# The scan of the odd layer in a two-block transformer kernel: block-diagonal tiles replaced by single 64 x 64 products on quarters of TensorE

## The chip, the cores and the metric

The program runs on one core of a Trainium2 chip. The metric is the device time of one execution in microseconds (us). The engines are TensorE (PE, with its weight loads as PEld), VectorE (DVE), ScalarE (ACT), GpSimd (POOL) and SyncE (SP, which issues the DMAs). The order of each engine's instructions is fixed when the program is built; between engines they wait on semaphores.

## What is computed

Two blocks of two layers follow each other, 512 tokens of x and 256 of context, 1024 features. The layer that matters here is the odd layer of the first block. Half of its mixer is an RWKV-7 recurrence over 8 heads of 64 features, once forward and once backward, first over the context and then, from the state that this leaves, over x:

```python
def wkv7_scan(state0, p, d, reverse, emit):
    ...
    def step(S, inp):
        w_t, k_t, v_t, kk_t, a_t = inp[:5]
        sa = jnp.einsum('bhvk,bhk->bhv', S, kk_t)
        S = (S * w_t[:, :, None, :] - sa[..., None] * (kk_t * a_t)[:, :, None, :]
             + v_t[..., None] * k_t[:, :, None, :])
        return S, (jnp.einsum('bhvk,bhk->bhv', S, inp[5]) if emit else None)
```

The decay `w_t` and the rate `a_t` come from low-rank products of the tokens; the outputs of both directions are added, normed per head, and gated (`rwkv7_readout`). Both kernels compute this in chunks of 64 tokens: within a chunk the steps become triangular 64 x 64 matrices per head, one of which has to be inverted, and between chunks only the 64 x 64 state passes.

## The kernel before, in words

`odd` runs the layer: the neighbourhood attention, then `rwkv_inputs` (projections, left in DRAM as `kap_d`, `k_d`, `r_d`, `vtok_d`), then `rwkv` (L1360), which holds the scan and the output product behind it. `others` gives steps of the output product of the attention half (`more`), matmuls of L414 on 512 columns, which `rwkv` spreads over the start of the scan.

**Units.** One unit is one chunk of one direction: 12 chunks (4 of context, 8 of x) times 2 directions, 24 units, each over all 8 heads. A unit is a generator, `pre` and then `serial`, that gives up its turn at every `yield`. The loop at the end of the scan goes by ticks: at every sixth tick a new unit joins, and in every tick each live unit does its next step. This order, as the tile framework's scheduler then refines it, is the order on the engines. A unit has 19 steps, so about three are live.

**Layouts.** Eight 64 x 64 matrices (one per head) are either a stack, tile [128, 4, 64], two heads on the two partition halves, or the diagonal blocks of a bd tile [128, 4, 128] whose other blocks stay zero. `prod` multiplies four stacked pairs by four bd tiles: stationary 128 x 64, moving 128 x 128. So an operand of the next product must be written into a bd tile, by two instructions of 64 partitions each (`expand` at L1401, on ACT or POOL; L1516, L1521, L1543 and L1552 likewise). `turn` (L1417) transposes a stack by two products with the identity.

**One unit.** `pre` loads kap, k and r of its 64 tokens, makes decays and scaled keys on POOL, DVE and ACT (tiles `ld`, `L`, `E`, `em`, `av`, `b`, `kd`, all 256 columns wide; the running sum is L1457), the low-rank products (L1446, tanh in `th`) once per two chunks. It then forms A (L1489) and the first inverse X (L1493, L1494), B, rk, rb, kt and bt, and inverts by five doubling levels: X is transposed to T (L1417, L1502), A is multiplied by X (masked into `bdw`, L1543), T by that, and half of X is updated (L1549) and copied to its bd tile (L1552). `values` loads the tokens' values three ways. `serial` takes the state N: products with E and B give `bdr` (L1582, L1583), X times it gives `un` (L1588), `kt` and `bt` give the new state (L1595 to L1604), and for x the output goes to `y`.

**Memory for results.** PSUM holds six one-bank tiles `rw` for `pre` and two `mm` for `serial`. At the start every bd tile is cleared (L1386, on POOL and DVE).

**After the scan** `readout` norms and gates the outputs; its first half starts at tick 141, beside the last units, the rest after them; the output product of this half follows.

Of the kernel before, what the change touches and what calls it, by code (L numbers as in the profile page):

```python
# [18 lines left out]
KD = 8  # L19
# [12 lines left out]
# ---------------------------------------------------------------- layouts made on the host  # L32
# [16 lines left out]
def _rows(w):  # L49
    """output features on partitions: [tile, P, contraction]"""  # L50
    return np.ascontiguousarray(w.T.reshape(-1, P, w.shape[0]))


def _consts():
# [24 lines left out]
    c["rscan"] = c["scan"][:, :256]  # L79
# [159 lines left out]
# ---------------------------------------------------------------- the program  # L239
# [7 lines left out]
def chain(products):  # L247
    """one step sequence: what comes after each product runs beside the steps of the next"""
# [11 lines left out]
def weave(base, other, per=1):  # L260
    """all steps of both: per steps of base, then one of other"""
# [11 lines left out]
class Prog:  # L273
# [16 lines left out]
    def xs(self, k, seg):  # L290
        """feature tile k of the residual stream, columns (first, number)"""
# [3 lines left out]
    def load_c(self, name, pool):  # L295
        """a tile of small vectors or constants, found by their names"""
# [16 lines left out]
    def psum(self, es, **bufs):  # L313
        """PSUM pools of a stage: mm one-bank tiles, s2 two-bank tiles"""
# [6 lines left out]
    def weights(self, side):  # L321
        """the pool of weights, which stages share so that loads run ahead of a stage's end"""
# [3 lines left out]
    def sbuf(self, es, side="left"):  # L326
        """scratch pool of a stage"""
# [5 lines left out]
    # ---- splitting into two float32r parts: hi + lo == value exactly  # L333
# [14 lines left out]
    def mm3(self, outs, w, acts, kt):  # L348
        """outs[i] (+)= w^T act_i over kt contraction tiles, exact float32r parts; w and acts give (hi, lo)."""
# [11 lines left out]
    def dense(self, dr, kt, act, segs):  # L361
        """feature-major product: one 128-column tile of weights dr [P, kt, P]; PSUM outputs per segment."""
# [3 lines left out]
    def dense_pair(self, drs, kt, act, segss, wide=False, by_seg=False):  # L366
        """column tiles whose products alternate over the contraction tiles, as these become ready, for all segments or
# [2131 lines left out]
```

## Time and profile before

| | us |
|---|---|
| median of 3 runs | 4167.52 |
| lowest and highest | 4164.29, 4172.4 |
| span of the profiled execution | 4163.7 |
| first A of the scan (L1489) to the last | 1389.8 to 1792.2 |
| last `un` (L1588) | 1824.2 |

No run's time is noted for the profiled execution apart from its span, which lies 3.8 us below the median of the runs. A profile row names line, engine and operation; a matmul of 32-bit floats of the program stands in it as two rows of weight load and two of matmul. "128*64 128x128" reads: 128 rows and 64 columns of the array, output of 128 columns on so many partitions. Busy time of PE counts from a row's start to its modelled end, and rows overlap.

### The profile page before, as it was taken

To read this page: it belongs to the slowest core of one execution; us is meant where nothing else is said; L and a number is where in the kernel's file an instruction comes from. 1 tells how busy PE (TensorE), PEld (TensorE's weight loads), DVE (VectorE), ACT (ScalarE), POOL (GpSimd) and SP (SyncE) were. 2 spreads that over 40 slices of the span, in tenths; PEclk is the share of its full clock that TensorE was granted. 3 is DMA by queue.
4 is the path that set the end of the run, shared out by engine and by line. 5 is a ranking of instruction groups with operands and counts; after the bars stand their busy time and mean duration, and the time that the engine had idled before them with its cause. 6 is when DMAs were issued, how large, how long until landed. Compare 5 with 4: busy or idle time off the path is not lost.

```text
span 4163.7 us, 61873 instructions
## 1 busy us (share of the span) xinstructions
PE 3961.8 (95%) x24688; PEld 3214.3 (77%) x24688; DVE 2477.5 (60%) x4382; ACT 1674.3 (40%) x3238; POOL 362.2 (9%) x439
## 2 busy tenths in 40 slices
PE   7899999999999999989999998999999899989998
PEld 5677888888777677768887877888887667767887
DVE  6556555545645676776766355555457888785334
ACT  4456321212544465553224252312125577663222
POOL 0222000000010221200000000000000231220000
PEclk8999999999999999999999998999999999999999
DMA  4220233323123211134553111233333223322232
GB/s 172 87 87 32 77 112 117 119 95 100 55 84 134 72 38 44 42 105 141 177 162 99 56 48 62 91 112 115 103 113 115 97 97 121 102 81 81 92 96 86
DMA packets 187888, 397.53 MB, mean 95 GB/s; under 512 B 80336, under 2 KB 89424, under 8 KB 186704
## 3 DMA queue, kind: packets, MB, share of 16 engines
q1 hardware_dynamic: 187600, 393.58, 29.4%
q8 instruction: 195, 3.19, 0.3%
q14 instruction: 93, 0.76, 0.1%
HBM read 379.23 MB, written 14.29 MB: 95 GB/s over the span
## 4 chain that ended last, share of the span: by engine, by line
PE 48%; DVE 5%; ACT 2%; issue 1%; POOL 0%; DMA 0%; DVEq 0%; ACTq 0%; POOLq 0%
PE mm L414 11%; PE mm L355 10%; PE mm L357 10%; PE mm L359 10%; PE mm L384 2%; PE y L2372 1%; DVE cva L2098 1%; DVE wlo L336 1%; PE seg L2170 0%; PE gl L1977 0%; ACT whi L335 0%; DVE y L2297 0%; DVE yl L2301 0%; DVE ch L2341 0%; PE mm L1412 0%
## 5 line engine op out<-in xcount | busy, mean ns | idle before, releaser
L335 ACT CAST whi<-w 128x1024 fp32r<-128x1024 f32 (+2 forms) x429 | 439.2, 1025 | 1582.4 <-PE mm L357 1008.3
L336 DVE TENSOR_TENSOR wlo<-w,whi 128x1024 fp32r<-128x1024 f32 (+2 forms) x429 | 517.6, 1207 | 329.6 <-ACT whi L335 320.8
L355 PE MATMUL mm<-fhi,whi 128*128 128x512 f32 x2016 | 610.0, 356 | 0.0
L357 PE MATMUL mm<-flo,whi 128*128 128x512 f32 x2016 | 609.4, 356 | 0.0
L359 PE MATMUL mm<-fhi,wlo 128*128 128x512 f32 x2016 | 607.5, 355 | 0.0
L359 PEld LDWEIGHTS mm<-fhi,wlo 128*128 128x128 f32 x2016 | 331.3, 187 | 61.4
L355 PEld LDWEIGHTS mm<-fhi,whi 128*128 128x128 f32 x2016 | 331.4, 187 | 60.7
L357 PEld LDWEIGHTS mm<-flo,whi 128*128 128x128 f32 x2016 | 331.4, 187 | 59.3
L471 DVE SCALAR_TENSOR_TENSOR wdot<-wmod,cb 128x1024 f32<-128x1024 f32 x288 | 352.0, 1222 | 10.8 <-ACT cb L465 3.6
L622 DVE SCALAR_TENSOR_TENSOR x<-mm,mod,x 128x512 f32<-128x512 f32 (+1 forms) x214 | 131.9, 642 | 325.5 <-PE mm L359 268.7
L734 DVE TENSOR_TENSOR g<-g,mm 128x512 f32<-128x512 f32 (+1 forms) x134 | 75.5, 590 | 405.1 <-PE mm L359 396.7
L355 PE MATMUL mm<-ah,whi 128*128 128x512 f32 x972 | 294.0, 356 | 0.0
L357 PE MATMUL mm<-al,whi 128*128 128x512 f32 x972 | 293.8, 356 | 0.0
L359 PE MATMUL mm<-ah,wlo 128*128 128x512 f32 x972 | 293.0, 355 | 0.7 <-DVE wlo L336 0.7
L359 PEld LDWEIGHTS mm<-ah,wlo 128*128 128x128 f32 x972 | 159.7, 187 | 30.7 <-DVE wlo L336 1.1
L834 POOL TENSOR_SCALAR p<-p,st 128x256 f32<-128x256 f32 (+3 forms) x128 | 95.7, 748 | 1008.3 <-DVE st L833 913.2
L355 PEld LDWEIGHTS mm<-ah,whi 128*128 128x128 f32 x972 | 159.7, 187 | 29.4
L357 PEld LDWEIGHTS mm<-al,whi 128*128 128x128 f32 x972 | 159.7, 187 | 28.7
L414 PE MATMUL mm<-shi,whi 128*128 128x512 f32 x328 | 138.9, 424 | 0.2 <-DVE x L2254 0.2
L414 PE MATMUL mm<-shi,wlo 128*128 128x512 f32 x328 | 130.6, 400 | 2.0 <-DVE wlo L336 2.0
L414 PE MATMUL mm<-slo,whi 128*128 128x512 f32 x328 | 131.8, 402 | 0.0
L2098 DVE SCALAR_TENSOR_TENSOR cva<-cvb,v_ssd,cva 128x512 f32<-128x512 f32 (+1 forms) x176 | 121.0, 701 | 11.0 <-ACT cva L2096 8.8
(598 smaller groups left out, 7957.7 us busy)
## 6 DMA issues: line engine op xcount, KB each, us to landing
wmod<-wmod SPq DMA_DIRECT2D x176, 512.0 KB, 3.7
w<-wfi SPq DMA_DIRECT2D x176, 512.0 KB, 3.3
w<-ws_in SPq DMA_DIRECT2D x62, 512.0 KB, 3.4
w<-wfo SPq DMA_DIRECT2D x64, 448.0 KB, 3.4
w<-wfo SPq DMA_DIRECT2D x32, 512.0 KB, 3.5
rb<-acd SPq DMA_DIRECT2D x32, 512.0 KB, 4.1
w<-wo_in SPq DMA_DIRECT2D x26, 512.0 KB, 3.3
w<-wa_in SPq DMA_DIRECT2D x21, 512.0 KB, 3.3
```

Source lines behind the costliest of these rows:

```text
L335: self.nc.scalar.copy(hi, src)
L336: (engine or self.nc.vector).tensor_tensor(out=lo, in0=src, in1=hi.bitcast(F32), op=ALU.subtract)
L355: nc.tensor.matmul(o, whi(k), ah(k), start=s, stop=False)
L357: nc.tensor.matmul(o, whi(k), al(k), start=False, stop=False)
L359: nc.tensor.matmul(o, wlo(k), ah(k), start=False, stop=e)
L384: self.nc.tensor.matmul(o, w[:, k], x[:, k, t0:t0 + n], start=s, stop=e)
L414: self.nc.tensor.matmul(o, w[:, k], x[:, k, t0:t0 + n], start=s, stop=e)
L471: dot = nc.vector.scalar_tensor_tensor(out=t, in0=w, scalar=1.0, in1=cb[:, i], op0=ALU.mult, op1=ALU.mult, accum_out=out[:, j, i:i + 1])
L622: self.nc.vector.scalar_tensor_tensor(out=x, in0=ps, scalar=mod[:, i_g + m, i:i + 1], in1=x, op0=ALU.mult, op1=ALU.add)
L734: nc.vector.tensor_tensor(out=g, in0=g, in1=u_, op=ALU.mult)
L834: nc.gpsimd.tensor_scalar(out=p, in0=p, scalar1=l, scalar2=1.0, op0=ALU.mult, op1=ALU.mult)
L2098: nc.vector.scalar_tensor_tensor(out=acc, in0=pc[:, t:t + n], scalar=w(t), in1=acc, op0=ALU.mult, op1=ALU.add)
```

## The change

All of it is within the scan of `rwkv`, and one constant (`rscan`, the marks at which the running sum starts anew, is 512 columns wide instead of 256).

- There are no bd tiles. `prod` takes single 64 x 64 matrices: stationary 64 x 64 on one half of the array's rows and one half of its columns, moving 64 columns (32 or 128 in places). The two halves of the rows write to different PSUM banks, so a result is a pair of banks; there are three such pairs and one ring for all products of the scan. Eight products go out as two groups of four that lie on the four quarters.
- A stack has three layouts (N, T, J), which say which bit of the head's number is the partition half. A product takes two layouts and gives the third kind; `seen` is the view of the result in the order of the target's tile.
- Decays and keys are made by `block` for two chunks at once, 512 columns wide, 9 ticks ahead of the first unit that needs them. Values come in one layout (`vj`), two DMAs per block.
- The five level masks of A are applied at once on POOL (`Al`, 1280 columns). X's transpose and A times X come as one result (`tw`, 64 + 32 columns per head: only the half of X's columns that changes), copied by one ACT instruction.
- B for x holds the strict and the inclusive products in one instruction of 512 columns; kt holds both transposes.
- B times the values is made ahead (`bv`), and the state's part is taken off it on DVE.
- A unit joins at every fourth tick and has 18 steps. The readout's first half starts when step 9 of both directions is done.

```diff
-            pps = self.pool(es, "rwps", 6, space=PSUM)
+            pps = self.pool(es, "rwps", 3, space=PSUM)
...
-            bank = lambda: pps.tile([P, 512], F32, tag="rw", name="rw")
+            LAY = {"N": (2, 0, 1), "T": (1, 0, 2), "J": (0, 1, 2)}
+            pair = lambda: pps.tile([P, 1024], F32, tag="rw", name="rw").rearrange("p (b c) -> p b c", b=2)
...
-            def prod(ps, *terms):
-                for g in range(4):
-                    o = ps[HALF[g % 2], P * (g // 2):P * (g // 2) + P]
-                    for i, (L, Rb) in enumerate(terms):
-                        nc.tensor.matmul(o, L[:, g], Rb[:, g], start=i == 0, stop=i == len(terms) - 1)
+            def prod(ps, lam, mu, *terms, base=0, step=64, at=0, n=64):
+                lb, mb = LAY[lam][0], LAY[mu][0]
+                bits = [0, 0, 0]
+                for bits[3 - lb - mb] in range(2):
+                    for i, (L, Rb) in enumerate(terms):
+                        for bits[lb] in range(2):
+                            for bits[mb] in range(2):
+                                g = 2 * bits[LAY[lam][1]] + bits[LAY[lam][2]]
+                                h = HALF[bits[lb]]
+                                o0 = base + step * bits[3 - lb - mb] + at
+                                nc.tensor.matmul(ps[HALF[bits[mb]], bits[lb], o0:o0 + n], L(g)[h], Rb(g)[h],
+                                                 start=i == 0, stop=i == len(terms) - 1)
+            def seen(ps, lam, mu, base=0, step=64, at=0, n=64):
+                v = ps[:, :, base:base + 2 * step].rearrange("p b (s w) -> p b s w", s=2)[:, :, :, at:at + n]
+                return v if LAY[mu][1] == LAY[lam][0] else v.rearrange("p b s w -> p s b w")
...
+                Al = up.tile([P, 5, 4, 64], F32, tag="Al", name="Al", bufs=3)
+                nc.gpsimd.tensor_tensor(out=Al, in0=A.unsqueeze(1).to_broadcast([P, 5, 4, 64]),
+                                        in1=mk[:, d, 1:6].unsqueeze(2).to_broadcast([P, 5, 4, 64]), op=ALU.mult)
...
                 for l in range(1, 6):
-                    Ti = inverse_t()
-                    pw = bank()
-                    prod(pw, (A, bx))
-                    W = bd("w")
-                    for h in range(2):
-                        nc.vector.tensor_tensor(out=on(W, h), in0=stack(pw)[HALF[h]], in1=mask(1 - d, l)[HALF[h]], op=ALU.mult)
+                    ps = pair()
+                    prod(ps, "T", "J", (grp(X), eye), step=96)
+                    prod(ps, "T", "J", ((lambda g: Al[:, l - 1, g]), (lambda g: blk(X[:, g]))), step=96, at=64, n=32)
+                    tw = sm("tw", 3, 96)
+                    nc.scalar.copy(two(tw), seen(ps, "T", "J", step=96, n=96))
                     yield
-                    pd = bank()
-                    prod(pd, (Ti, W))
+                    ps = pair()
+                    prod(ps, "J", "T", ((lambda g: tw[:, g, 0:64]), (lambda g: tw[:, g, 64:96])), step=32, n=32)
...
-                    if l < 5:
-                        for h in range(2):
-                            nc.scalar.copy(blk(on(bx, h)), blk(X[HALF[h]]))
+                    nc.vector.tensor_tensor(out=xb, in0=xb, in1=s, op=ALU.subtract)
                     yield
...
-                if todo and tick % 6 == 0:
-                    live.append(todo.pop(0))
+            EVERY, AHEAD = 4, 9
+            for i in range(12):
+                for d in range(2):
+                    t0 = AHEAD + EVERY * (2 * i + d)
+                    if i % 2 == 0:
+                        start.setdefault(t0 - AHEAD, []).append((block, d, chunk(d, i) // 2))
+                    start.setdefault(t0, []).append((unit, d, i))
```

On PE, in the middle of the scan, the order before (names: `bdx`, `bdw`, `bdb` are bd tiles, `consts` holds the identity):

```order
L1412 MATMUL rw<-bdb_12126,E 64x128 x4
L1412 MATMUL rw<-bde_12099,b 64x128 x4
L1417 MATMUL rw<-consts,X 128x128 x2
L1412 MATMUL mm<-bdr_12110,X 64x128 x3
L1412 MATMUL rw<-bdx_12123,A 64x128 x4
L1509 MATMUL rw<-E,bdk_12128 128x128 x4
L1519 MATMUL rw<-E,bdb_12126 128x64 x4
L1412 MATMUL mm<-bdr_12110,X 64x128
L1412 MATMUL rw<-bdw_12119,T 64x128 x4
```

and the order now (`c_odd` holds the identity of 64):

```order
L1394 MATMUL rw<-tw 64x32 x16
L1438 MATMUL mm<-ru,lora 128x128
L1394 MATMUL rw<-tw 64x32 x8
L1394 MATMUL rw<-E,kd 64x128 x8
L1394 MATMUL rw<-E,b 64x64 x8
L1394 MATMUL rw<-N,E 64x64 x8
L1394 MATMUL rw<-c_odd,X 64x64 x8
L1394 MATMUL rw<-X,Al 64x32 x8
```

Products of four matmuls on 128 rows have become products of eight on 64 rows; only the low-rank products (L1438) still use all rows, and they stand singly between the others.

On DVE, a stretch of the same place before:

```order
L1543 TENSOR_TENSOR bdw_12119<-rw,rmask 64x4x64 x2
L1543 TENSOR_TENSOR bdw_12120<-rw,rmask 64x4x64 x2
L1465 TENSOR_TENSOR E<-E,kx 128x4x64
L1467 TENSOR_TENSOR b<-b,em 128x256
L1468 SCALAR_TENSOR_TENSOR kd<-av,vecs 128x256
L1481 TENSOR_TENSOR E<-E,rr 128x4x64
L1471 SCALAR_TENSOR_TENSOR kd<-kd,kk 128x256
L1549 TENSOR_TENSOR X<-X,rw 128x4x32
L1472 TENSOR_TENSOR kd<-kd,em 128x256
L1549 TENSOR_TENSOR X<-X,rw 128x32x4
```

and now, with a block's instructions in it:

```order
L1496 TENSOR_TENSOR B<-rw,rmask 128x512
L1501 TENSOR_TENSOR rb<-rw,rmask 128x256
L1541 TENSOR_TENSOR bv<-bv,rw 128x256
L1461 SCALAR_TENSOR_TENSOR kd<-av,vecs 128x512
L1462 TENSOR_TENSOR E<-E,kx 128x8x64
L1463 TENSOR_TENSOR b<-b,em 128x512
L1465 SCALAR_TENSOR_TENSOR kd<-kd,kk 128x512
L1468 TENSOR_TENSOR kd<-kd,em 128x512
L1534 TENSOR_TENSOR X<-X,rw 128x8x16
L1534 TENSOR_TENSOR X<-X,rw 128x32x4
```

The masked copies into bd tiles are gone, and the work on decays and keys stands in runs of five or six instructions of 512 columns between those that empty PSUM.

## Rows read from the trace of the kernel before

**Rows 1.** the page: span, and busy time of each engine over the whole program

```profile
span 4163.7 us, 61873 instructions
PE 3961.8 (95%) x24688; PEld 3214.3 (77%) x24688; DVE 2477.5 (60%) x4382; ACT 1674.3 (40%) x3238; POOL 362.2 (9%) x439
```

**Rows 2.** lines L1489 and L1588: ns min/median/max, first and last start, forms

```profile
L1489 ACT COPY A<-rw x24: 372/372/373, 1389.8 to 1792.2; 128x256 f32<-128x256 f32 x24
...
L1588 ACT COPY un<-mm x24: 353/372/373, 1420.9 to 1824.2; 128x256 f32<-128x256 f32 x24
```

**Rows 3.** busy time by stretch: before the first unit, first to last, the rest

```profile
core 0: us, PE busy (x) PEld busy (x) DVE busy (x) ACT busy (x) POOL busy (x), PEclk, DMA share, GB/s
1364.50:1389.80 25.30, 21.82 (x108) 16.43 (x108) 17.23 (x31) 8.43 (x16) 13.60 (x27) 1.00 0.60 163
1389.80:1792.20 402.40, 374.63 (x4173) 301.10 (x4172) 289.26 (x734) 238.42 (x678) 83.41 (x147) 1.00 0.17 39
1792.20:1824.20 32.00, 29.64 (x298) 22.00 (x297) 20.67 (x54) 16.55 (x46) 0.00 (x0) 0.95 0.22 61
```

**Rows 4.** waits, 1389.8 to 1792.2: total us, times, longest us

```profile
ACT bdx L1552 <- DVE X L1549: 34.3, 30, 2.6
DVE N L1603 <- PE mm L1597: 32.7, 18, 2.3
...
ACT T L1502 <- PE rw L1417: 23.4, 35, 1.5
```

**Rows 5.** timeline of PE, gated linear attention: start, us, line, tiles, shapes, rows

```profile
2490.30 0.28 PE L1928 MATMUL gl<-gvt,kt 64*64 64x128 f32 x2
2490.33 0.28 PE L1952 MATMUL tp<-qd,kn 64*64 64x64 f32 x4
2490.41 0.28 PE L1928 MATMUL gl<-gvt,kt 64*64 64x128 f32 x2
2490.45 0.28 PE L1952 MATMUL tp<-qd,kn 64*64 64x64 f32 x4
2490.52 0.28 PE L1928 MATMUL gl<-gvt,kt 64*64 64x128 f32 x2
...
2535.94 0.64 PE L1952 MATMUL tp<-qd,kn 64*64 64x64 f32 x16
```

**Rows 6.** timeline in the scan: a product that fills the array

```profile
1611.99 1.16 PE L1509 MATMUL rw<-E,bdk 128*128 128x128 f32 x8
```

**Rows 7.** VectorE by line: ns min/median/max, first and last start, forms

```profile
L1549 DVE TENSOR_TENSOR X<-X,rw x120: 279/289/294, 1395.5 to 1822.7; 128x128 f32<-128x128 f32 x120
L1493 DVE TENSOR_TENSOR X<-rw,rmask x24: 407/425/427, 1389.5 to 1792.0; 128x256 f32<-128x256 f32 x24
...
L1457 DVE TENSOR_TENSOR_SCAN L<-c_odd,ld x24: 684/692/882, 1384.2 to 1771.6; 128x256 f32<-128x256 f32 x24
...
L1458 DVE TENSOR_TENSOR ld<-L,ld x24: 410/436/735, 1385.5 to 1774.7; 128x256 f32<-128x256 f32 x24
```

**Rows 8.** VectorE by line and shape, whole program: busy us, mean ns, idle before

```profile
L1249 DVE TENSOR_TENSOR zs<-zc 128x512 f32<-128x512 f32 x14 | 9.6, 687 | 8.6 <-ACT zc L1247 8.6
```

**Rows 9.** ScalarE, the same view

```profile
L886 ACT COPY pt<-tp 128x384 f32<-128x384 f32 x64 | 30.5, 477 | 56.4 <-PE tp L883 56.0
...
L1448 ACT ACTIVATE th<-rw 128x512 f32<-128x512 f32 x24 | 14.2, 597 | 2.9 <-PE rw L1446 2.0
...
L1532 ACT COPY bt<-rw 128x512 f32<-128x512 f32 x22 | 12.9, 585 | 1.1
...
L563 ACT ACTIVATE rs<-rs 128x512 f32<-128x512 f32 x6 | 3.8, 631 | 0.2
```

**Rows 10.** GpSimd, the same view

```profile
L2159 POOL TENSOR_TENSOR xw<-xt,dtw 128x512 f32<-128x512 f32 x40 | 52.0, 1304 | 816.0 <-ACT xt L2124 793.2 <-PE seg L2170 20.7 <-PE tp L2289 1.8
...
L834 POOL TENSOR_SCALAR p<-p,st 128x512 f32<-128x512 f32 x32 | 23.1, 721 | 761.1 <-DVE st L833 737.3 <-DVE st L825 8.9 <-DVE mod L502 4.7
```

**Rows 11.** busy time by stretch: the end of the gated linear attention

```profile
2541.50:2565.00 23.50, 18.19 (x118) 13.98 (x117) 10.89 (x26) 5.74 (x16) 0.00 (x0) 0.50 0.21 68
```

More of the change, by code (lines that the diff above doesn't have):

```diff
@@ L78, in _consts @@
     t = np.arange(64)
-    c["rscan"] = c["scan"][:, :256]
+    c["rscan"] = c["scan"][:, :512]
     c["i64"] = np.tile(np.eye(64), (2, 1))
@@ L1421, in chunk @@
+            eye = lambda g: i64
+            state, blocks, done = {0: None, 1: None}, {}, set()
             def chunk(d, i):
@@ L1493, in pre @@
-                nc.vector.tensor_tensor(out=X, in0=stack(ps), in1=mask(1 - d, 0), op=ALU.mult)
-                nc.vector.tensor_tensor(out=X, in0=i64, in1=X, op=ALU.subtract)
-                expand(bx, X, (nc.scalar, nc.scalar))
-                yield
-                def inverse_t():
-                    ps = bank()
-                    turn(ps, X)
-                    Ti = sm("T", 3)
-                    nc.scalar.copy(Ti, stack(ps))
-                    return Ti
-                ps = bank().rearrange("p (q t) -> p q t", q=4)
@@ L1507, in pre @@
[L1507 to L1521 removed]
+                yield
@@ L1522, in pre @@
                 yield
                 if i < 11:
-                    ps = bank()
-                    turn(ps, kd)
-                    u["kt"] = sm("kt", 3)
-                    nc.scalar.copy(u["kt"], stack(ps))
-                    ps = bank().rearrange("p (q t) -> p q t", q=4)
-                    for p in range(4):
-                        nc.tensor.transpose(ps[:, p], bb[:, p], ident)
-                    u["bt"] = up.tile([P, 4, P], F32, tag="bt", name="bt", bufs=3)
-                    nc.scalar.copy(u["bt"], ps)
@@ L1619, in unit @@
-            def unit(d, i):
-                yield from pre(d, i)
-                yield from serial(d, i)
+                    ps = pair()
+                    prod(ps, "N", "T", (grp(N), e1))
+                    prod(ps, "J", "T", (v, (lambda g: B[:, g, 64:P])), (grp(un), grp(rb)), base=P)
+                    c4 = ci - 4
+                    yy = two(y[:, :, 64 * c4:64 * c4 + 64])
+                    if (c4 < 4) == (d == 0):
+                        nc.scalar.copy(yy, seen(ps, "N", "T"))
+                    else:
+                        nc.vector.tensor_tensor(out=yy, in0=yy, in1=seen(ps, "N", "T"), op=ALU.add)
@@ L1624, in readout @@
+                    nc.vector.tensor_tensor(out=yy, in0=yy, in1=seen(ps, "J", "T", base=P), op=ALU.add)
+                done.add((d, i))
             def readout(cols, yh, yl):
@@ L1635, in readout @@
                     yield
-                    pv = two(bank())
+                    pv = halves(self.bank())
                     nc.tensor.matmul(pv, self.c("bd64"), sq, start=True, stop=True)
@@ L1644, in readout @@
                     yield
-            todo = [unit(d, i) for i in range(12) for d in range(2)]
-            live, tick = [], 0
-            while todo or live:
-                if todo and tick % 6 == 0:
-                    live.append(todo.pop(0))
-                live = [u for u in live if next(u, todo) is not todo]
-                if tick in (1, 3):
-                    clear(2 if tick == 1 else 0, (nc.gpsimd,))
+            EVERY, AHEAD = 4, 9
+            start = {}
+            for i in range(12):
[4 more added lines that the diff above has]
+                    start.setdefault(t0, []).append((unit, d, i))
+            live, tick, reading = [], 0, False
+            while start or live:
+                live += [f(*at) for f, *at in start.pop(tick, ())]
+                live = [u for u in live if next(u, start) is not start]
                 if tick < 15:
@@ L1658, in rwkv @@
                     run(more)
-                elif tick == 141:
+                elif reading:
+                    next(more, None)
+                elif (0, 9) in done and (1, 9) in done:
+                    reading = True
                     yh, yl = parts()
@@ L1662, in rwkv @@
                     more = readout(slice(1, 3), yh, yl)
-                elif tick > 141:
-                    next(more, None)
                 tick += 1
```

279 lines of the change are left out of this document (118 added, 161 removed).

## Prediction

> **What bounds the kernel now.** I read the page first, then the scan alone. Over the program PE is busy 95% of the span [rows 1], but that mean belongs to the dense products and says nothing of the scan. Where the scan lies is told by two lines that occur once per unit: A is copied 24 times, first at 1389.8 us and last at 1792.2, and the last `un` starts at 1824.2 [rows 2]. Between the first and the last A lie 23 steps of 402.4 / 23 = 17.5 us. The reader is to see in the table by stretch [rows 3] that no engine is full there: DVE is busy 289.3 of 402.4 us (72%, 12.6 us per unit) and ACT 238.4 (59%, 10.4 us per unit). PE shows 374.6, but that counts each row to its modelled end: its 4173 rows, mostly half-array rows, stream in far less. The waits [rows 4] agree: ACT waits for DVE, DVE for PE, ACT for PE, none above 34.3 of 402 us. It is a loop in which about three units hand results from PE to ACT or DVE and back. So its pace follows the sum of what the fullest engine has to do, times a factor for the waiting: 12.6 us of DVE work make 17.5 us.
>
> **The change, part by part.** The counts are those of the two programs' instructions in the scan; durations are those of rows.
>
> *DVE.* Removed are 240 masked copies into `bdw`, 64 into `rk` and `rb`, and half of those of `bdr` and `bdn`. What stays: 160 instructions of 256 columns at 0.425 us (as L1493 in [rows 7]), 68.0; 120 updates of X at 0.289 [rows 7], 34.7; 16 of B and 80 of the blocks, 512 columns at 0.687 [rows 8], 66.0; 12 running sums of 512 columns, not in the trace, at most twice the 0.692 of 256 [rows 7], 16.6. Together 185.3. GpSimd will be busier (below), and the 256-column L1458 shows what a neighbour can do: least 0.410, median 0.436, most 0.735 [rows 7]. I add twice the 6% between least and median to the 66.0, 8 us; the worst row would add 52. That makes 193 us, **8.0 us per unit** against 12.6.
>
> *ACT.* 72 copies of 256 columns (A, bv, un) at 0.372 [rows 2], 26.8; 22 of kt at 0.585, 120 of `tw` at 0.477 (its width is that of L886), 24 tanh at 0.597 and 32 exponentials at 0.631 [rows 9], together 104.6; 8 of `y`, 3.0. That is 134, **5.6 us per unit** against 10.4. Gone are the copies into `bdx`, `bdb`, `bdk`, `bdr` and T.
>
> *PE.* Now 5232 products on quarters, two rows each, 10464 rows or 436 per unit. The scan has no such row, but the gated linear attention has. There 16 rows of 64 columns on two quarters of the same partition half take 0.64 us [rows 5]; less the 0.22 of a last row's end this is 0.42 / 14 = 0.030 us per row. Where both halves work, 2 + 4 + 2 + 4 rows start from 2490.30 to 2490.52 [rows 5], 0.018 each, a third of them twice as wide. So four quarters do run at once, and I take half of 0.030: 157 us, plus 3 for 256 rows of 128 columns. Rows of 32 columns still load 64 columns of weights, so I give them no gain. The 24 groups of low-rank products fill the array, at 1.16 each [rows 6], 28. That is 188, **7.8 us per unit**; at 0.030 it would be 347, 14.5.
>
> *POOL.* 24 masks of A of 1280 columns, from 1.304 for 512 [rows 10] some 3.26 each, 78; 24 scalings at 0.721 [rows 10], 17; 12 products at 1.304, 16. That is 111, 4.6 us per unit, below the others, though one mask follows a block's three instructions and may be late for the first level, by some 2 us per block at worst (3.26 + 1.30 + 0.72 against two ticks); DVE's backlog covers that.
>
> *Nothing, and what hides it.* The 25 clearings on POOL and six on DVE ran beside the products before the first unit, where PE is busy 21.8 of 25.3 us [rows 3]. These products of `more` still stand ahead of the first unit, and a block's longer chain waits beside them, so I leave the first A at 1389.8, give or take 5. The loads fall from 188 to 56 DMAs of the same or fewer bytes; the queue was not awaited and a block is loaded 9 ticks ahead. The readout and the output product keep their work.
>
> *The pace.* DVE (8.0) and PE (7.8) are now nearly level. At the share of before, 8.0 / 0.72 = 11.1 us. A second way: before, the pace lay between DVE alone, 12.6, and DVE and ACT one after the other, 23.0, at (17.5 - 12.6) / 10.4 = 0.47 of the way; now 8.0 + 0.47 * 5.6 = 10.6. Three pairs of PSUM banks instead of eight single ones let PE run ahead by three products only, and the blocks' runs of five or six wide instructions on DVE (some 4 us) hold back the copies behind them, so I take the upper one, 11.0. The ends are 8.0 (DVE never waits) and 13.6 (ACT and DVE never overlap).
>
> *The sum.* Last A: 1389.8 + 23 * 11.0 = 1642.8. From there to the last `un` before: 14 ticks of 17.5 / 6, 40.8 us at full pace, took 32.0 [rows 3], 0.78 of it. Now 15 ticks of 11.0 / 4 are 41.3, times 0.78 = 32.2. The last `un` is at 1675.0 instead of 1824.2: 149.2 us less. The span of 4163.7 [rows 1] becomes 4014.5; the median of the runs lies 3.8 above the span, so **4018 us**. In the same way 8.0 gives 3940 and 13.6 gives 4086.
>
> [...] The rows show twelve starts in 0.22 us [rows 5], one each 18 ns. [...]
>
> **Rivals.**
>
> 1. *Two rows at a time* (slower than before). The four quarters do not get going together: in `prod` the four matmuls of a group write to two banks, accumulate in turn, and wait on results that come singly, so that the rate is that of the 16 rows, 0.030 us each [rows 5]. PE then needs 14.5 us per unit and is the fullest engine: at the share of 0.72 a pace of 20.1, last `un` at 1389.8 + 462.3 + 58.8 = 1910.9, 87 us later: 4254. It decides from a pace of 16.8 on (23 + 15 / 4 * 0.78 = 25.9 paces make 434.4 us), which PE reaches at 12.1 us per unit, 0.025 us per row; if PE never waited, 14.5 would give 4109. For it: the rows of 64 columns mostly come in twos. Against it: the mixed stretch. 10%, of which 6 slower. [...]
>
> 2. *The clock.* [...] If half of the scan ran at half clock, PE would need 11.7 us per unit, at 0.72 a pace of 16.3: 1389.8 + 374.9 + 47.7, 12 us less than before, 4156. 9%.
>
> 3. *ACT and DVE in turn.* The unit's steps come in such an order that a tick's copies are all ACT's (three `tw` and A) or all DVE's (y, three X, B, rb), and the three bank pairs let neither work while the other does. Then the pace is 13.6, 4086. For it: the PSUM ring is the only store between PE and both. Against it: four or five live steps per tick from different units, and the blocks' work needs no PSUM. This is the upper part of my own case; with it that case has 78%.
>
> The last 3% are for what none of these covers.
>
> **How the numbers follow.** 4018 is the likeliest case's own value. Its ends, 3940 and 4086, hold the unknown rate of the quarters and the sharing between GpSimd and DVE; the upper one is moved to 4110 to take in rival 1 where PE never waits, and what of rival 2 lasts shorter. Some 8 in 10 lie between. About 0.2%, 8 us, is what a measurement of this kernel can tell from no change: slower by more has the 6% of rival 1 and 2% of the clock; within it lie 4%, of rival 2 mostly; faster by more has 88%.
>
> **What would show it.** In the changed kernel's lines: A 24 times some 11 us apart, the last about 1643, the last `un` about 1675; DVE some 190 us busy between, about 70%, ACT half; 16 rows of a quarter product within 0.4 to 0.5 us; a granted clock of 1.00. It is wrong in the pace if A comes 8 or 14 us apart: then the busy shares say whether an engine filled up or bank pairs were awaited (PE waiting for the copy of the product three before). Rival 1 shows as 16 rows in 0.6 us and as waits of DVE and ACT for PE's products; rival 2 as a clock of 0.50 in the scan's stretches. If the first A is later than 1395, the start was mispriced.

## The result and the profile after

The changed kernel takes **4120.99 us** (median of 4 runs, 4116.48 to 4126.67) where the kernel before takes 4167.57 (4164.29 to 4172.4): the ratio is 0.9887, 95% interval 0.9873 to 0.9901. It is faster by some 47 us. The forecast of 4018 (3940 to 4110) had the sign; the gain is under a third of the 149 us expected.

The page of the changed kernel, span and busy time (as [rows 1]):

```profile
span 4124.9 us, 72730 instructions
PE 3850.0 (93%) x30860; PEld 3149.4 (76%) x30860; DVE 2395.2 (58%) x3988; ACT 1551.8 (38%) x2814; POOL 376.9 (9%) x322
```

Its lines for A and `un` (as [rows 2]):

```profile
L1485 ACT COPY A<-rw x24: 367/372/379, 1397.5 to 1739.5; 128x256 f32<-128x256 f32 x24
...
L1546 ACT COPY un<-rw x24: 372/378/379, 1443.2 to 1773.6; 128x256 f32<-128x256 f32 x24
```

Busy time by stretch (as [rows 3]): before the first unit, first to last A, up to the last `un`, and from there to the output product:

```profile
core 0: us, PE busy (x) PEld busy (x) DVE busy (x) ACT busy (x) POOL busy (x), PEclk, DMA share, GB/s
1364.00:1397.50 33.50, 23.67 (x133) 17.78 (x131) 17.41 (x27) 9.17 (x16) 5.95 (x6) 0.90 0.55 164
1397.50:1739.50 342.00, 257.78 (x9573) 234.12 (x9565) 206.10 (x345) 117.12 (x264) 104.74 (x53) 0.79 0.11 30
1739.50:1773.60 34.10, 28.90 (x1053) 23.52 (x1048) 19.80 (x50) 14.58 (x34) 2.89 (x1) 0.85 0.13 35
1775.00:1805.30 30.30, 18.16 (x40) 10.18 (x41) 12.90 (x28) 11.07 (x26) 0.00 (x0) 0.55 0.37 122
```

A unit now comes every 342.0 / 23 = 14.9 us, not every 11.0 (before: 17.5). Against the forecast span of 4014.5 the 110 us that are missing lie so: the first A is 7.7 us late, 23 paces are 3.87 us too long each (89.0), the tail is 1.9 longer, and behind the last `un` 11.8 are lost (4124.9 - 1773.6 = 2351.3, before 4163.7 - 1824.2 = 2339.5): the readout runs at a granted clock of 0.55 there (0.88 in the 30 us behind the last `un` before). So the loss is in the pace for the most part. VectorE is busy for 206.1 us, 9.0 per unit, 60% of the stretch; no engine is full, again. The clock stands at 0.79 where it stood at 1.00.

Where VectorE's time went, by line in that stretch (busy us, mean ns, idle time before):

```profile
L1490 DVE TENSOR_TENSOR X<-c_odd,X 128x256 f32<-128x256 f32 x23 | 55.1, 2397 | 0.3
...
L1447 DVE TENSOR_TENSOR_SCAN L<-c_odd,ld 128x512 f32<-128x512 f32 x10 | 12.2, 1224 | 37.3 <-POOL ld L1444 37.3
L1461 DVE SCALAR_TENSOR_TENSOR kd<-av,vecs 128x512 f32<-128x512 f32 x10 | 12.0, 1200 | 0.0
L1452 DVE TENSOR_TENSOR ld<-L,ld 128x512 f32<-128x512 f32 x10 | 11.7, 1174 | 0.0
L1489 DVE TENSOR_TENSOR X<-rw,rmask 128x256 f32<-128x256 f32 x23 | 9.5, 414 | 31.4 <-PE rw L1394 31.4
```

L1489 and L1490 have one shape, 256 columns. The first reads PSUM and takes 0.41 us; the second reads two operands in SBUF and takes 2.40. The timeline of one unit shows why (rows of PE left out):

```profile
1520.37 2.88 POOL L1504 TENSOR_TENSOR Al<-A,rmask 128x1280 f32<-128x1280 f32 x1 [10.52 <-ACT A L1485]
...
1520.57 0.29 DVE L1534 TENSOR_TENSOR X<-X,rw 128x128 f32<-128x128 f32 x1 [0.17 <-PE rw L1394]
1520.78 2.76 DVE L1490 TENSOR_TENSOR X<-c_odd,X 128x256 f32<-128x256 f32 x1
...
1523.46 0.47 DVE L1534 TENSOR_TENSOR X<-X,rw 128x128 f32<-128x128 f32 x2
```

GpSimd's mask `Al` ends at 1523.25, the subtraction at 1523.54. In 20 of the 23 units the subtraction ends 0.3 us after the `Al` that it met. In the other three, which met none, it takes 0.41 to 0.42. L1534, with one operand in PSUM, runs through beside the mask in 0.29. So in these rows the subtraction, with two operands in SBUF, is held until the mask that it meets is done: 2.40 us in the mean against 0.41.

### The profile page after: what moved, and what is told of

Its sections match the earlier page's. It is cut to its first block, busy times and chain, and to the rows that moved or that the text cites. A ratio compares the mean times of both kernels' runs of the same rounds, so it can differ in the third digit from the quotient of the medians.

```text
span 4124.9 us, 72730 instructions
## 1 busy us (share of the span) xinstructions
PE 3850.0 (93%) x30860; PEld 3149.4 (76%) x30860; DVE 2395.2 (58%) x3988; ACT 1551.8 (38%) x2814; POOL 376.9 (9%) x322
## 3 DMA queue, kind: packets, MB, share of 16 engines
q8 instruction: 242, 3.96, 0.4%
## 4 chain that ended last, share of the span: by engine, by line
PE 52%; DVE 8%; ACT 3%; issue 2%; POOL 0%; DMA 0%; DVEq 0%; ACTq 0%; SPq 0%; POOLq 0%
PE mm L414 11%; PE mm L355 10%; PE mm L357 10%; PE mm L359 10%; PE rw L1394 4%; PE mm L384 3%; PE y L2327 1%; DVE X L1490 1%; DVE wlo L336 1%; DVE cva L2053 1%; PE seg L2125 0%; PE gl L1932 0%; PE mm L1438 0%; DVE ch L2296 0%; ACT whi L335 0%
```

## The experiments

Each ratio is to the kernel before, run on the same chip. That kernel took 4165.8 to 4172.9 us on the chips used, so kernels of different chips are compared by their ratios. Pace is from the first to the last A; clock and VectorE's busy time are those of that stretch, in one execution of each kernel. For the mask on VectorE that execution, 4091.5 us, was the slowest of four, so paces some 0.5 us apart are not told from each other.

| kernel | us | ratio, 95% interval | pace us | clock | DVE us |
|---|---|---|---|---|---|
| the change | 4121.0 | 0.9887 (0.9873 to 0.9901) | 14.9 | 0.79 | 206 |
| X from PSUM | 4103.7 | 0.9854 (0.9839 to 0.9868) | 14.1 | 0.86 | 173 |
| mask in five pieces | 4102.7 | 0.9848 (0.9832 to 0.9865) | 14.0 | 0.88 | 167 |
| **mask on VectorE** | 4080.0 | 0.9799 (0.9781 to 0.9816) | 13.25 | 0.89 | 185 |
| change + filling products | 4124.6 | 0.9902 (0.9887 to 0.9916) | 14.9 | 0.90 | 210 |
| change + later running sum | 4115.7 | 0.9875 (0.9860 to 0.9890) | 14.7 | 0.82 | 206 |
| X from PSUM + later sum | 4111.1 | 0.9863 (0.9846 to 0.9879) | 14.2 | 0.87 | 173 |
| mask on VectorE, and: | | | | | |
| - unit every 3 ticks | 4097.7 | 0.9826 (0.9812 to 0.9841) | 13.1 | 0.88 | 187 |
| - filling products | 4104.5 | 0.9847 (0.9832 to 0.9861) | 14.1 | 0.95 | 191 |
| - four PSUM pairs | 4087.4 | 0.9813 (0.9797 to 0.9830) | 13.4 | 0.89 | 186 |
| - two PSUM pairs | 4123.2 | 0.9897 (0.9882 to 0.9912) | 14.6 | 0.79 | 196 |
| - thin blocks | 4075.1 | 0.9779 (0.9759 to 0.9798) | 12.9 | 0.94 | 158 |
| - tw in bfloat16 | 4072.6 | 0.9761 (0.9747 to 0.9776) | 12.6 | 0.83 | 192 |
| - 32 tiny products | 4123.7 | 0.9886 (0.9872 to 0.9901) | 14.8 | 0.84 | 187 |
| - turns as transposes | 4393.5 | 1.0539 (1.0521 to 1.0556) | 25.8 | 0.59 | 182 |
| - tw in bfloat16, `more` spread | 4069.5 | 0.9763 (0.9748 to 0.9777) | 13.1 | 0.86 | 194 |
| before + 32 tiny products | 4231.5 | 1.0157 (1.0140 to 1.0174) | 20.2 | 0.94 | 298 |

### Is it GpSimd's hold on VectorE?

**X from PSUM.**

```diff
-vector.tensor_tensor(out=two(X), in0=seen(ps), in1=mask(1 - d, 0), op=mult)
-vector.tensor_tensor(out=X, in0=i64s, in1=X, op=subtract)
+vector.tensor_tensor(out=seen(ps), in0=seen(ps), in1=mask(1 - d, 0), op=mult)
+vector.tensor_tensor(out=two(X), in0=i64q, in1=seen(ps), op=subtract)
```

> Edit: the masked product is written back into its PSUM pair, and X is formed from that, so that VectorE's second instruction for X reads one operand from PSUM and one from SBUF, not two from SBUF. GpSimd's mask of A (Al) stays as it is. Theory 'lock' (VectorE's subtraction of two SBUF operands waits until GpSimd's Al ends, 2.4 us in the mean instead of 0.42; PE starves behind it and its clock falls afterwards): the subtraction takes some 0.42 us, VectorE's sum between the first and the last A falls from 206 to some 161 us, the granted clock there rises from 0.79 to over 0.93, the pace falls from 14.9 to 12 to 12.8 us, and the time is 4055 to 4080. Theory 'short rows' (rows on quarters keep PE too little at work for the full clock, whatever VectorE does): the subtraction gets short as well, but the clock stays at 0.75 to 0.85, the pace at 14 to 14.9, and the time is 4100 to 4121.

VectorE loses 33 us, the time 17: 4103.7 lies in the range of 'short rows', not of 'lock'. The subtraction is short, but by line, in the same stretch, another instruction with two SBUF operands now meets the mask:

```profile
L1453 DVE TENSOR_TENSOR ld<-L,ld 128x512 f32<-128x512 f32 x10 | 25.8, 2577 | 0.0
...
L1448 DVE TENSOR_TENSOR_SCAN L<-c_odd,ld 128x512 f32<-128x512 f32 x10 | 12.2, 1224 | 34.0 <-POOL ld L1445 34.0
```

The hold has moved to `ld` (2.58 us; 1.17 in the changed kernel).

**Mask in five pieces.** One instruction of 1280 columns on GpSimd becomes five of 256, each in its own tile.

> Edit: GpSimd's one mask of 1280 columns (2.9 to 3.9 us) becomes five of 256 columns, each in a tile of its own; VectorE's instructions stay. Theory 'lock': VectorE waits for one piece at most (about 0.7 us by the 256 columns' share of the 3.3), the subtraction takes 0.42 to 1.2 us in place of 2.4, and the time is 4060 to 4090. Theory 'short rows': the subtraction gets shorter too, the clock stays near 0.79, time 4100 to 4121. If the lock is handed over only when GpSimd's queue is empty, nothing changes: 4121.

The subtraction falls to 0.63 us in the mean, the time by 18 us, again into the range of 'short rows'. The hold has moved here too: `E` at L1462 takes 1.46 us in the mean.

**Mask on VectorE.** `nc.gpsimd.tensor_tensor(out=Al, ...)` becomes `nc.vector.tensor_tensor(out=Al, ...)`.

> Edit: the mask of A goes from GpSimd to VectorE, in one instruction of 1280 columns. Theory 'lock': the subtraction takes 0.42 us, the mask itself some 1.7 us on VectorE (128 columns 0.28, 512 columns 0.68, so about 0.10 us per 100 columns), VectorE's sum is some 200 us as now, but nothing waits for GpSimd; clock over 0.88, time 4080 to 4105. Theory 'short rows': VectorE does no less than now and the clock stays, 4115 to 4135.

By line of VectorE in the scan:

```profile
L1504 DVE TENSOR_TENSOR Al<-A,rmask 128x1280 f32<-128x1280 f32 x23 | 34.6, 1503 | 56.1 <-ACT A L1485 56.1
...
L1447 DVE TENSOR_TENSOR_SCAN L<-c_odd,ld 128x512 f32<-128x512 f32 x10 | 12.2, 1220 | 1.3 <-POOL ld L1444 1.3
...
L1490 DVE TENSOR_TENSOR X<-c_odd,X 128x256 f32<-128x256 f32 x23 | 10.4, 454 | 0.1
```

Best of the three, though VectorE now does the mask as well (1.50 us against 3.32 on GpSimd): the subtraction takes 0.45 us, and VectorE no longer stands before the running sum for `ld` (1.3 us in place of 37.3). The time falls by 41 us, into the range of 'lock', and the clock rises to 0.89, which 'short rows' excluded.

But two things changed at once. VectorE's wait for `ld` in the changed kernel did not come from a queue on GpSimd:

```profile
1532.93 0.60 ACT L1439 ACTIVATE th<-mm 128x512 f32<-128x512 f32 x1 [0.58 <-PE mm L1438]
...
1533.61 0.62 POOL L1444 TENSOR_SCALAR ld<-th 128x512 f32<-128x512 f32 x1 [10.36 <-ACT th L1439]
...
1534.26 1.22 DVE L1447 TENSOR_TENSOR_SCAN L<-c_odd,ld 128x512 f32<-128x512 f32 x1 [3.24 <-POOL ld L1444]
```

GpSimd had been idle for 10.36 us and began `ld` some 0.09 us after the end of the tanh that it reads, and so in all ten blocks of the stretch. VectorE stood because its order has the running sum ahead of the time when low-rank product and tanh are done. With the mask on VectorE the rest of its order is another as well, and the wait is gone. So the 41 us are the price of the hold and of this order together. Loosening the hold alone gave 17 and 18 us, with the wait for `ld` still there (34.0 and 36.9 us). The hold is shown, by three ways of loosening it; its share of the 41 us is not.

**Later running sum.** One more `yield` ahead of the running sum, on the change and on X from PSUM.

> Edit: in the block's preparation the running sum on VectorE (L1447 of the changed kernel) comes one tick later than GpSimd's scaling of ld that it reads; Al stays on GpSimd, and so does the lock on the subtraction. In the changed kernel VectorE stood 37 us in 10 waits for ld, since ld queues on GpSimd behind an Al. Theory 'queue' (VectorE, held at the running sum, holds the copies behind it): those waits fall under 10 us, and the time falls by 10 to 25 us from 4121, to 4096 to 4111. Theory 'lock alone': VectorE would have stood elsewhere in that time, 4115 to 4125.

> Edit: X formed from PSUM (as in the first experiment, 4104) and the running sum one tick later, with Al still one mask on GpSimd. Theory 'lock and queue' (the mask on GpSimd costs the scan by these two ways and by nothing else): together they give what moving the mask to VectorE gave, 4065 to 4085. If only one of them matters: 4095 to 4105. Theory 'short rows': the clock stays at half for 70 us or more of the scan, and the time over 4090.

Neither tests its theory: VectorE still waits 34.7 and 34.3 us for `ld`, presumably since the framework's scheduler sets the order anew. The edit did not do what it says, so the 4115.7 us in the range of 'lock alone' say nothing. The second kernel's 4111.1 us are in the range of 'short rows' alone, with a clock of 0.87. A queue on GpSimd, which the first text gives as the cause, is not what the rows above show.

### Is it the clock?

```diff
+fl = self.bank()
+for _ in range(2):
+    nc.tensor.matmul(fl, lora[:, 0, 0, 0:P], lora[:, 0, 1], start=True, stop=True)
```

> Edit: behind each unit's second product (the one for X) PE gets two more full-array float32 products of 512 columns into a spare bank that nothing reads; nothing else changes, so the output is the same. They take about 0.85 us each at full clock, 40 us of PE in the scan. Theory 'lock': the subtraction still takes 2.4 us and still ends with Al, the pace stays above 14, time 4100 to 4140, whatever the clock does. Theory 'short rows': the clock rises over 0.93 and PE, freed from half clock, gives a pace of 12 to 13.5, time 4060 to 4095 in spite of the added work.

> Edit: the mask of A on VectorE (4080) and two more full-array products of 512 columns behind each unit's second product, into a bank nothing reads. Half clock then still took 68 us of the scan. Theory 'clock': the clock rises to 0.96 or more and the pace falls to 11.5 to 12.5, time 4045 to 4070. Theory 'latency': the clock rises, but PE is not what is waited for, and the added work (1.7 us per unit) takes PE away from others: pace 13 to 14, time 4075 to 4105.

On the change the clock rises from 0.79 to 0.90 and the pace stays at 14.9: if the higher clock gave anything, the added products took it. Without the hold it rises from 0.89 to 0.95 and the kernel gets 24 us slower. Of the 20 times that the clock fell to half in the change's scan, 17 lie within 2 us of the end of an `Al`. That fits a clock that falls because PE has run dry behind the hold; shown is only that holding it up with idle work brings nothing. Nor do the rows on quarters by themselves hold it at 0.79, as 'short rows' had it: the same rows run at 0.89 with the mask on VectorE and at 0.94 with thin blocks.

### What sets 13.25 us, with the hold gone?

VectorE is busy 185.2 us of 304.8, of which the mask is 34.6; its other work is 6.5 us per unit in this stretch. The pace is 13.25 all the same, not 11.0. Four things were tried.

**A unit every 3 ticks** (`EVERY` 3 in place of 4).

> Edit: the mask of A on VectorE (4080) and a new unit every 3 ticks in place of 4, so that about six units are under way instead of four. Theory 'latency' (no engine is full: PE starts rows in 131 of 305 us, VectorE is busy 185, ACT 116; a tick lasts as long as the chain of one step, about 3.3 us): the pace falls by up to a quarter, from 13.25 to 10.5 to 11.5 us, and the time to 4025 to 4050. Theory 'in order' (VectorE and PE are held by their own queues, one late step holding all others): the tick grows as the steps in it do, pace 12.3 to 13.3, time 4065 to 4085.

**PSUM pairs.** Four: the ring gets the banks of `mm`, and `self.bank()` takes the first bank of a pair. Two: the ring's 3 becomes 2.

> Edit, on the kernel with the mask of A on VectorE (4080 us, pace 13.25): four pairs of PSUM banks in place of three; the two single banks of the low-rank products, of `more` and of the readout are given up, these take the first bank of a pair from the same ring. Theory 'ring' (a product starts only when the product three before has been copied out; a unit takes a pair about 20 times, and if each is held 1.7 to 2 us, three pairs give 11 to 13 us per unit): the pace falls to 10 to 11.5 us and the time to 4025 to 4050, perhaps 10 us more since `more` holds pairs at the start. Theory 'engines' (VectorE's order of work and PE's own sequence set the tick; another pair only waits longer): pace 12.8 to 13.5, time 4070 to 4090.

> Edit, on the kernel with the mask of A on VectorE: two pairs of PSUM banks in place of three, all else the same. Theory 'ring': the pace goes with the number of pairs, 17 to 20 us, time 4165 to 4235, slower than before the change. Theory 'engines': pace under 14.5, time under 4110.

**Thin blocks.** Six wide instructions of the blocks work on 8 of 64 columns.

> Edit, on the kernel with the mask of A on VectorE: six of the wide instructions of a block's preparation on VectorE work on 8 of 64 columns (64 per partition in place of 512) and leave the rest of their results out; the scaling of av is made 100 times smaller to keep the numbers bounded. VectorE loses some 0.55 us in each of 68 instructions, 36 of its 185 us. Theory 'bursts' (VectorE's runs of wide instructions, some 6 us per block, hold the copies behind them): pace 10.8 to 12, time 4020 to 4055. Theory 'ring' with a hold that has other causes: pace 12.4 to 13, time 4060 to 4075. Theory 'load' (pace goes as VectorE's sum, at the share 0.61): 6.5 / 0.61 = 10.7 us.

**Four pairs and a unit every 3 ticks.**

> Edit, on the kernel with the mask of A on VectorE: four pairs as in the first of these runs and a new unit every 3 ticks in place of 4. With three pairs the shorter distance changed the pace from 13.25 to 13.06 only. Theory 'ring': with more pairs the shorter distance counts too, pace 9.5 to 10.5, time 4005 to 4035. Theory 'engines': as with four pairs alone, or up to 20 us more as at three pairs (4098 against 4080).

The shorter distance alone takes the pace to 13.1 but lengthens the tail, and costs 18 us, more than either theory had. A fourth pair brings nothing (13.4), though it also has to serve the low-rank products, and with units every 3 ticks it brings nothing either (4101.0). A pair less costs 1.3 us per unit, a fraction of what the ring would make it; its 4123.2 us lie between the two theories. With thin blocks 27 us less on VectorE bring 0.35 us per unit and 5 us of time, within the spread of the runs (4065 to 4081). Ring, latency, bursts and VectorE's load each fail as the one bound.

What these runs share is in PE's rows. The timeline of PE, mask on VectorE, in brackets the idle time and what the profile names as its end:

```profile
1629.47 0.41 PE L1394 MATMUL rw<-c_odd,X 64*64 64x64 f32 x16
1629.70 0.39 PE L1394 MATMUL rw<-X,Al 64*64 64x32 f32 x16
1629.91 0.44 PE L1394 MATMUL rw<-c_odd,X 64*64 64x64 f32 x16
1631.98 0.43 PE L1394 MATMUL rw<-X,Al 64*64 64x32 f32 x16 [1.63 <-issue]
1632.23 0.44 PE L1394 MATMUL rw<-c_odd,X 64*64 64x64 f32 x16
1632.49 0.39 PE L1394 MATMUL rw<-X,Al 64*64 64x32 f32 x16
1632.70 0.44 PE L1394 MATMUL rw<-b,E 64*64 64x64 f32 x16
1633.06 0.46 PE L1394 MATMUL rw<-E,b 64*64 64x64 f32 x16
1633.53 0.46 PE L1394 MATMUL rw<-E,N 64*64 64x64 f32 x16
1633.81 0.30 PE L1394 MATMUL rw<-B,vj 64*64 64x64 f32 x8
1633.93 0.30 PE L1394 MATMUL rw<-rb,un 64*64 64x64 f32 x8
1634.05 0.30 PE L1394 MATMUL rw<-B,vj 64*64 64x64 f32 x8
1634.16 0.30 PE L1394 MATMUL rw<-rb,un 64*64 64x64 f32 x8
1635.73 0.49 PE L1394 MATMUL rw<-tw 64*64 64x32 f32 x19 [1.27 <-ACT x L1568]
```

Between the two stops lie 6 x 16 + 4 x 8 = 128 matmul rows, and as many weight loads: 256 instructions, done in 2.5 us. Then PE stands for 1.3 us, as it had for 1.6 ahead of them, there in the middle of a level whose operands were long ready ("issue"); the second stop the profile puts down to a copy on ACT. The DMA view of the 25 us around it, in 40 slices: up to the loads in the last ones, all that moves is one packet of q8, an instruction queue, in each slice marked 26; that it is PE's is read from the counts below.

```profile
GB/s 0 0 0 0 0 26 0 0 0 0 0 26 0 0 0 0 0 26 0 0 0 0 26 0 0 0 0 0 0 26 0 0 0 116 208 136 175 3 8 8
```

The queue table of that view, now for the whole scan of the kernel before (packets, MB, share of the DMA engines' time):

```profile
q8 instruction: 34, 0.56, 0.6%
```

For the scan of the changed kernel:

```profile
q8 instruction: 75, 1.23, 1.5%
```

And with the mask on VectorE:

```profile
q8 instruction: 74, 1.21, 1.7%
```

1.23 MB / 75 are 16.4 KB, and the 19138 rows and loads of the changed kernel's scan are 255 per packet; with the mask on VectorE it is 259, with tw in bfloat16 256, with 32 tiny products 258, and in the kernel before 245. So q8 goes with PE's count, and a packet is taken as 256 instructions. Before, one came every 402.4 / 34 = 11.8 us; now every 4.6, and with the mask on VectorE every 304.8 / 74 = 4.1. No run here shows how many fetched instructions PE can hold, nor why it stops.

That it does stop at the fetches is seen when all stops are counted. With the mask on VectorE, PE's starts (rows and loads) come to lie over 0.4 us apart 71 times, 82 us together. Of these, 41 stops, 51 us, end 2 to 3 us after a fetch begins, though that is only a quarter of the time; and 32 of the 41 lie within 14 instructions of the same place in each 256, where 1 of the other 30 does. In the change it is 34 of 72 stops, 47 us; before the change 1 of 56. In the mean the fetches are 3.95 us or more apart in every run (thin blocks: 297.0 / 75 = 3.96), but that is no floor: single ones come as close as 3.2 us, and such a mean only says the pace once more, by 23 / 75.

So PE's instructions were taken away and added, on the kernel with the mask on VectorE.

**32 tiny products** of one column per unit, on quarters, into spare banks.

> Edit, on the kernel with the mask of A on VectorE: behind each unit's second product 32 more products on quarters with one moving column each, into spare banks that nothing reads: 128 PE instructions more per unit and some 0.9 us of PE's time. Theory 'instruction supply': pace higher by 128 / 256 * 4.1 = 2.05 us, 15.3, time 4120 to 4135. Theory 'work': by 0.5, time 4085 to 4100.

86 fetches, one every 340.1 / 86 = 3.95 us; the pace rises by 1.5 us, the time by 44. Against the kernel before on the same chip it is 37 (4172.9 - 4123.7 = 49.2 us gained, not 4165.8 - 4080.0 = 85.8), just under what the supply asks for (40 to 55) and over what the work does (5 to 20). The stretch is 35 us longer, of which 13 lie in stops that end 2 to 3 us after a fetch begins (64.5 us in place of 51.1). So the supply is not all of it.

**tw in bfloat16**, which rounds part of X: one row and one load per product in place of two.

> Edit, on the kernel with the mask of A on VectorE: the tile tw is bfloat16, so each of its 40 products per unit takes one matmul row and one weight load in place of two; X is updated with rounded numbers. 80 PE instructions less per unit. Theory 'instruction supply': pace lower by 80 / 256 * 4.1 = 1.3 us, 11.95, time 4042 to 4057. Theory 'work': 40 rows are 0.6 us of PE, pace lower by 0.3, time 4068 to 4080.

68 fetches; the pace falls by 0.6, between the 1.3 of the one theory and the 0.3 of the other. The time is 7 us lower, 15 against the kernel before on the same chip, between the theories too (23 to 38, and up to 12). The stops at fetches fall from 51 to 36 us, about as much as the stretch gets shorter (14 us); those elsewhere grow from 31 to 46 us, and the clock fell to 0.83: other waits take over as soon as the supply gives way. The supply is at most a part of what sets the pace.

**Turns as transposes**, half of the products with the identity.

> Edit, on the kernel with the mask of A on VectorE (4080 us, pace 13.25): of the products with the identity (turns of X and of kt), those that end on partitions 0 to 63 become PE transposes, which take one matmul row and one weight load for 32-bit data where a product takes two of each. Per unit PE has 56 instructions less of some 824, and 28 rows of matmul less. Theory 'instruction supply' (PE stops after every 256 instructions until the next 16 KB of them has come: 74 fetches in the 304.8 us of the scan, one each 4.1 us, whatever is done on the other engines): the pace falls by 56 / 256 * 4.1 = 0.9 us to 12.35, the time to 4052 to 4065, the fetches stay 4.0 to 4.1 us apart. Theory 'work' (PE's streaming time is what counts: 1.7 us more of it, in the run with the added products, cost 0.84 us per unit): 28 rows are 0.4 us, the pace falls by 0.2, time 4072 to 4082.

Both theories miss by over 300 us. The timeline of PE (L1396 are the transposes, L1398 the products):

```profile
1600.52 0.31 PE L1396 MATMUL rw<-c_odd,X 64*64 64x64 f32 x1
1600.76 0.47 PE L1398 MATMUL rw<-c_odd,X 64*64 64x64 f32 x2
1601.16 0.31 PE L1396 MATMUL rw<-c_odd,X 64*64 64x64 f32 x1
1601.40 0.47 PE L1398 MATMUL rw<-c_odd,X 64*64 64x64 f32 x2
```

A transpose and the two rows of the product beside it take 0.64 us, one after the other (0.24 from the transpose's start to the product's, 0.40 from there to the next transpose), where 16 rows on four quarters take 0.26 (1632.23 to 1632.49 above; 0.46 at half clock in the change); so one turn of X takes 2.56 us. The clock was at 0.59. Why the two do not run together no run shows. Added to tw in bfloat16, the turns cost as much:

> Edit: both of these together, 136 PE instructions less per unit of some 824. Theory 'instruction supply': pace lower by 136 / 256 * 4.1 = 2.2 us, 11.1, time 4020 to 4040, unless VectorE (8.05 us per unit) now holds it: then it ends near 11.5. Theory 'work': pace lower by 0.5, time 4062 to 4075.

It took 4402.0. The cost of the transposes hides what fewer instructions bring, and neither run says anything on the supply.

**The same 32 products in the kernel before**, where the supply is not short.

> Edit, on the kernel before the change: behind each unit's product for X, 32 more products with one moving column each (stationary 128 x 64, into a spare bank that nothing reads): 128 PE instructions more per unit, to some 490, and 1 to 2 us of PE's time. The same number cost 1.54 us per unit (44 us of time) on the kernel with the mask on VectorE. Theory 'instruction supply': before the change a fetch of 256 instructions was needed each 12 us only and now each 9 us, twice the 4 us that bind the changed kernel, so they cost under 0.6 us per unit: 4166 to 4182. Theory 'the added products themselves' (each costs PE or the others its time): 1.5 us per unit here too, 4195 to 4215.

It cost more, 2.7 us per unit. The control fails: the added rows run two at a time there, not four,

```profile
1501.02 1.98 PE L1494 MATMUL mm<-b,c_odd 128*64 128x1 f32 x64
```

so from the first start to the last they take 1.8 us of PE's line in a unit at best, over 3 in 12 of the 24, and 2.8 in the mean, and that kernel passes nearly all of it on. Both theories miss (4231.5). That the tiny products cost their 1.5 us by their fetches is thus not shown apart from their work; that PE stops at fetches is shown by its rows.

**The best of them**, `more` one step per tick up to tick 60, with tw in bfloat16.

> Edit: mask of A on VectorE, tw in bfloat16 (4073 us, rounds part of X), and the steps of `more` one per tick up to tick 60 in place of three per tick up to tick 15, so that some 48 products of 512 columns go from before the first unit to beside the first units. They are 11 us of PE. Theory 'instruction supply' and 'latency': they are few instructions (under 100 of 256 per fetch) and fit where PE stands still; the first A comes up to 8 us earlier, time 4062 to 4072. Theory 'work': they cost beside the units what they save ahead of them, 4070 to 4078.

The first A comes at 1391.3, the pace gives most of it back. 4069.5 us is the lowest time seen, but the ratio, 0.9763 against 0.9761 without the spread, shows no gain; it rounds part of X. With float32 and all of the work the fastest is the mask on VectorE, 4080.0, which beats the change and the kernel before.

## Why the prediction was right or wrong

- **The sign and the counts** were right. Summed by line over all 24 units, ACT took 137 us for 134, GpSimd 114 for 111 (one mask 3.30 for 3.26), and VectorE 189 for 185 (in the kernel with the mask on VectorE, the mask left out).
- **PE's rows** were right in size: 16 rows of 64 columns in 0.26 us and of 32 columns in 0.21 (1632.23 to 1632.70 above), 0.013 to 0.016 each for the 0.015 taken, at the full clock (in the change 16 rows of 32 columns take 0.21 us at a granted clock of 1.00 and 0.39 at 0.50). Four quarters do run at once.
- **"I add twice the 6% between least and median to the 66.0, 8 us; the worst row would add 52."** This step failed. It spread the neighbour's cost over the blocks' wide instructions, where it was nearly right (67.2 us for 80 of them in the change, 12 more than at 0.687 each), and missed that the second instruction for X reads two SBUF operands just when GpSimd masks the A of the same unit. L1490 alone took 55.1 - 23 * 0.414 = 45.6 us more. Loosening this hold gave back 17 of the 103 us in the time; taking the mask off GpSimd, which also took VectorE's wait for `ld` away, 41.
- **"At the share of before, 8.0 / 0.72 = 11.1 us."** This step failed too, and for more: with the mask off GpSimd the missing 2.25 us per unit are still 52 us. It set a count of all 24 units (193 / 24 = 8.0) against the busy time of a stretch (289.3 / 23 = 12.6); summed like the first, the kernel before has 324 / 24 = 13.5. And it carried a share of waiting from one loop to another. With the mask on VectorE and left out, VectorE's work fills 150.6 of the 304.8 us of the stretch, 0.49, where it filled 0.72 before. The sum had no term for PE's instructions: 363 per unit became over 830 (matmuls and loads of [rows 3] and above, by 23), and PE's stops at their fetches are 51 us there, 47 in the change, where before there was one. That these stops are the missing 52 us is not shown: other waits took over part of what fewer instructions freed.
- **"The readout and the output product keep their work"**: they do, but at a granted clock of 0.55, mostly half clock, and 11.8 us are lost there; the first A came 7.7 us late, outside the 5 allowed.
- **Rival 1**, two rows at a time, has the wrong mechanism. That its case "if PE never waited", 4109, lay nearest is luck: its 0.030 us per row happens to be close to 128 rows per fetch at the mean distance, 3.96 / 128 = 0.031.
- **Rival 2**, the clock, came true in the rows: 0.79, with 143 of the 342 us at half clock, the 0.50 of [rows 11]. Whether it is a cause of the pace or a result of PE's waits is not shown; raising it with added products brought nothing.
- **Rival 3**'s ring got nothing from a fourth pair, though it lost 1.3 us per unit without the third.

Open stays how supply, clock and waits share what is left between 11.0 and 13.25 us; no run took PE's instructions alone by half.

## What to carry to other kernels

Price a GpSimd instruction also by what VectorE does beside it: list VectorE's instructions with two SBUF operands that follow the same releaser (here 2.40 us in place of 0.41 for one of them). When a change makes many small PE instructions of few large ones, count them, matmuls and loads, and look for stops of PE behind the fetches on its instruction queue (here 41 stops, 51 of 304.8 us), before asking how fast the rows stream. Look at what each wait waits for before naming its cause: VectorE's wait for `ld` came from the tanh ahead of it, not from GpSimd's queue. A share of waiting measured in one loop is no property of the next.

## What the runs showed that was not expected

- PE stops again and again where 256 instructions are done in some 2.5 us: with the mask on VectorE 41 stops, 51 of 304.8 us, end 2 to 3 us after a fetch begins. Single fetches came as close as 3.2 us apart, in the mean of a run no closer than 3.95.
- A transpose on one quarter next to a product on another costs 0.64 us, at a granted clock of 0.59 in the mean, and took the kernel to 4393 us.
- In the kernel before, tiny products that take 2.8 us of PE's line per unit in the mean cost 2.7 us per unit, though the profile shows no full engine there: its loop hung on PE's line more than the waits [rows 4] told.
